# Keeping the split projection weights of a hybrid decoder block in DRAM between row blocks

## The chip, the core and the metric

The kernel runs on one core of a Trainium2 chip. A core has five engines that run their own instruction streams in order and meet at semaphores: PE (TensorE, matrix products), DVE (VectorE), ACT (ScalarE), POOL (GpSimd) and SP (SyncE), which here issues nearly all DMAs from one in-order queue. The metric is device time in microseconds (us) of a whole execution. The kernel before takes 1531.31 us, the median of three runs (1530.76, 1531.31 and 1535.02).

## The reference

One layer (DEPTH is 1) over 2048 rows of 1024 columns, in float32. What matters here is that all three mixers read one combined projection, with a weight matrix of 1024 rows and 4232 columns:

```
h = rms_norm(x, norm_g) * (1 + scale[:, None]) + shift[:, None]
proj = h @ w_in                       # 2048 x 1024 times 1024 x 4232
(ga_u, ga_v, ga_z, mb_q, mb_k, mb_v, mb_o, mb_z, mb_i, mb_f,
 sc_q, sc_k, sc_v, sc_z) = jnp.split(proj, offsets, axis=-1)
y_a = spatial_gating_branch(...) * silu(ga_z)      # gMLP, 4 groups of 64
h_b = mlstm_branch(...)                            # mLSTM, 4 heads of 96
y_c = stick_breaking_branch(...) * silu(sc_z)      # 6 heads of 64, strictly causal
y = jnp.concatenate([y_a, y_b, y_c], axis=-1) @ w_out
return x + gate[:, None] * y
```

The stick-breaking attention needs, for each query row, a running product over all earlier keys, so its work grows with the row's place in the sequence.

## The kernel before, in words

A row block is 5, 5 and 6 tiles of 128 rows (BLOCKS). For each block the normalised rows are turned once into hT, which holds a high part (float32 rounded to the PE's fp32r format) and a low part (what the rounding left). Then eleven groups of projection columns follow, of 384 columns each (392 for one): three for the attention (c_proj, p = 0 to 2), two for the mLSTM's q and k (bqk_proj), two for its gates (bg_proj), one each for its values (bv_proj) and the attention's gate (cz_proj), two for the gMLP (a_proj).

For every group of every block `weights` makes eight tiles "wr", one for 128 rows of w_in each, with a high and a low part. `load_w` fetches 256 rows into a staging tile "st" (two buffers). ACT copies each half into the high part (L180). Then DVE, for the even tile, or POOL, for the odd one, subtracts it from the staged values and so makes the low part (L181). A product of a tile of 128 rows is 8 steps of three matmuls (high by high, high by low, low by high), L285 to L287. The pool of "wr" tiles has 11 buffers: while one group is in use, three tiles of the next can be made ahead, and the tile of step k (from 3 on) has to wait until PE has done with step k - 3 of the group before, for the last row tile.

The attention of a pair of heads (`stick`) runs beside these groups: PE makes scores (L367, L368), ACT two sigmoids (L372, L373), DVE a running product (the scan, L380), DVE and POOL in turn a product (L384), PE turns it (L395), ACT and DVE split it (L397, L398), and PE multiplies by V (L410). The generators of `stick` are interleaved with those of the projections, and a scheduler puts the instructions of each engine into a fixed order by its own model of their times and by priorities; the weight work of later blocks has a high priority (HIGH is -4000). An engine runs its order without overtaking. K and V of the earlier blocks are kept in DRAM (k_d, v_d) and loaded again for each pair of heads.

The low-part line is the one whose engine alternates:

```
(nc.vector if a == 0 else nc.gpsimd).tensor_tensor(
    wt[:, 1, :W], st[:, a, :W], wt[:, 0, :W].bitcast(F32), ALU.subtract)
```

Of the kernel before, what the change touches and what calls it, by code (L numbers as in the profile page):

```python
# [8 lines left out]
F32 = mybir.dt.float32  # L9
F32R = mybir.dt.float32r  # L10
# [5 lines left out]
DRAM = bass.MemoryType.DRAM  # L16

P = 128
# [6 lines left out]
WMAX = 392  # L25
# [7 lines left out]
def hybrid_block_kernel(ctx: ExitStack, tc: tile.TileContext, x, c, norm_g, w_ada, b_ada, w_in,  # L33
# [8 lines left out]

# [1 line left out]
    qkT_d = dram.tile([768, SEQ], F32, name="qkT_d")  # L44
# [9 lines left out]

# [1 line left out]
    ident = const.tile([P, P], F32, name="ident")  # L56
# [35 lines left out]

# [1 line left out]
    rs = ExitStack()  # L94
# [50 lines left out]
    def mod_x(i, c0, c1, eng=None):  # L145
        """normalised and modulated, in place"""
        xc = x_cols(i, c0, c1)
        nc.vector.scalar_tensor_tensor(xc, xc, xtiles[i][1], hscale[:, c0:c1], ALU.mult, ALU.mult)
        (eng or nc.gpsimd).tensor_tensor(xc, xc, hshift[:, c0:c1], ALU.add)
# [10 lines left out]

    ntag = [0]

    def load_w(src, segs, kp):
# [8 lines left out]
    def weights(src, segs, kps=range(KT // 2), staged=None):  # L172
        """hi and lo parts of the given columns, one tile per 128 rows"""
        W = sum(w for _, w in segs)
        tiles = []
        for kp in kps:
            st = staged[kp] if staged else load_w(src, segs, kp)
            for a in range(2):
                wt = wr_p.tile([P, 2, WMAX], F32R, tag="wr", name=f"wr{ntag[0]}_{kp}_{a}")
                nc.scalar.copy(wt[:, 0, :W], st[:, a, :W])  # L180
                (nc.vector if a == 0 else nc.gpsimd).tensor_tensor(  # L181
                    wt[:, 1, :W], st[:, a, :W], wt[:, 0, :W].bitcast(F32), ALU.subtract)
                tiles.append(wt)
        ntag[0] += 1
        return tiles
# [4 lines left out]

# [1 line left out]
    ht_p = lw.enter_context(tc.tile_pool(name="ht", bufs=1))  # L192
# [51 lines left out]

# [1 line left out]
    NB0 = BLOCKS[0]  # L246
# [22 lines left out]
    def hT_half(i, j, hh):  # L269
        """half of the rows of tile j of hT, hi and lo parts"""  # L270
        cols = slice(j * P, (j + 1) * P)
        ks = slice(hh * 4, hh * 4 + 4)
        pt = (pat.tile([P, 4, P], F32, tag="at", name=f"pt{i}_{hh}") if i < BLOCKS[0] else
              pproj.tile([P, 512], F32, tag="proj", name=f"pt{i}_{hh}").rearrange("p (k t) -> p k t", k=4))
        for k in range(4):
            kk = hh * 4 + k
            nc.tensor.transpose(pt[:, k, :], x_cols(i, kk * P, (kk + 1) * P), ident)
        nc.scalar.copy(hT[:, 0, ks, cols], pt)
        nc.vector.tensor_tensor(hT[:, 1, ks, cols], pt, hT[:, 0, ks, cols].bitcast(F32), ALU.subtract)  # L279

    def proj_tc(ps, wt, j, W, ks=range(KT)):
        """psum[t, cols] of t tile j of the block"""
        cols = slice(j * P, (j + 1) * P)
        for k in ks:
            nc.tensor.matmul(ps, lhsT=hT[:, 0, k, cols], rhs=wt[k][:, 0, :W], start=k == 0, stop=False)  # L285
            nc.tensor.matmul(ps, lhsT=hT[:, 0, k, cols], rhs=wt[k][:, 1, :W], start=False, stop=False)  # L286
            nc.tensor.matmul(ps, lhsT=hT[:, 1, k, cols], rhs=wt[k][:, 0, :W], start=False, stop=k == KT - 1)  # L287
            yield 3 * W / 2.4

# [1 line left out]
    def c_proj(b, t0, nb, p):  # L291
# [148 lines left out]

# [1 line left out]
    def bqk_proj(t0, nb, half):  # L442
# [71 lines left out]

# [1 line left out]
    def a_proj(t0, nb, p):  # L516
# [37 lines left out]

# [1 line left out]
    def gating():  # L556
# [62 lines left out]

# [1 line left out]
    def bc4(ap, n):  # L621
# [31 lines left out]
    def first_chunk():  # L653
        """chunk 0 of the mLSTM ahead of the output phase: its gated output and the state after it"""
        big = [tmp.tile([P, D], F32, tag="xt", name=f"m0_{n}") for n in range(2)]
# [37 lines left out]

# [1 line left out]
    def gate_gemv():  # L695
# [137 lines left out]

# [1 line left out]
    rs.close()  # L835
# [46 lines left out]
    def mlstm(i):  # L882
        """numerator and denominator of chunk i, state after it"""
        qk2, vb = loaded[i][0:2]
        Cp = CT[0]
        wT = wk.tile([P, 4, P], F32, tag="wT", name=f"wT{i}")
        intra_weights(i, wT)
        pT = wk.tile([P, 4, P], F32, tag="pT", bufs=1, name=f"pT{i}")
        scores(psS.tile([P, 4, P], F32, tag="s", name=f"s{i}"), qk2, pT, wT)
        yield  # L890
        if i < NT - 1:
            kw = wk.tile([P, 4, 96], F32, tag="kw", bufs=1, name=f"kw{i}")
            weighted_k(i, psK.tile([P, 4, P], F32, tag="k", name=f"k{i}"), qk2, kw)
            yield
        ips = psI.tile([P, 4, P], F32, tag="i", name=f"i{i}")
        for h in range(4):
            nc.tensor.matmul(ips[:, h, 0:97], lhsT=qk2[:, h, :], rhs=Cp[:, h, :], start=True, stop=True)
        nd = wk.tile([P, 4, 97], F32, tag="nd", name=f"nd{i}")
        nc.vector.tensor_tensor(nd, ips[:, :, 0:97], bc4(ex[:, 0, 4 * i:4 * i + 4], 97), ALU.mult)
        yield  # L900
        nps = psN.tile([P, 4, P], F32, tag="n", name=f"n{i}")
        for h in range(4):
            nc.tensor.matmul(nps[:, h, 0:97], lhsT=pT[:, h, :], rhs=vb[:, h, :], start=True, stop=True)
        nc.vector.tensor_tensor(nd, nps[:, :, 0:97], nd, ALU.add)
        nds[i] = nd
        if i < NT - 1:
            yield
            cps = psK.tile([P, 4, P], F32, tag="k", name=f"c{i}")
            for h in range(4):
                nc.tensor.matmul(cps[0:96, h, 0:97], lhsT=kw[:, h, :], rhs=vb[:, h, :], start=True, stop=True)  # L910
            Cn = wk.tile([96, 4, 97], F32, tag="C", name=f"C{i}")
            nc.gpsimd.tensor_tensor(Cn, Cp, bc4(decay[0:96, 4 * i:4 * i + 4], 97), ALU.mult)
            nc.vector.tensor_tensor(Cn, cps[0:96, :, 0:97], Cn, ALU.add)
            CT[0] = Cn

    def mixed(i):
        """the gated outputs of the three mixers, [t, c]"""
        gt, y, xt = loaded[i][2:]
# [42 lines left out]
    def chunk_ahead(i):  # L961
        """chunk i from its scores to the turned outputs"""
        yield from mlstm(i)
        mixed(i)
        yield
        yield from turned(i)
# [66 lines left out]
```

## Time and profile before

| | |
|---|---|
| runs (us) | 1531.31 median, 1530.76 to 1535.02 |
| span of the profiled execution | 1527.0 us (the execution's own time is not given beside it; the runs are 3.8 to 8.0 us longer than this span) |
| busy: PE, DVE, POOL, ACT | 1413.2, 1123.3, 757.2, 749.6 us |
| granted clock of PE, mean | 0.978 |
| chain that ended last, by engine | PE 53%, DVE 25%, issue 7%, DMA 6%, POOL 5%, ACT 4% |
| DMA | 163.89 MB, 107 GB/s over the span |
| HBM read, written | 124.58 MB, 37.64 MB |

Busy is the union of an engine's instructions; matmuls overlap, so a busy PE is not a PE at its peak. After a start of about 62 us the projections of block 0 run to 354 us, those of block 1 to 718 us and those of block 2 to 1216 us; the attention of block 2 ends at 1264 us, and the output projection follows. The stretches 62 to 356, 356 to 720 and 720 to 1265 us stand for the three blocks. The weight tiles of block 1 are made from about 345 us on but for the first few, so the work on weights in blocks 1 and 2 is read from 345 to 1265 us.

### The profile page before, as it was taken

The numbers are of one execution on the slowest core, as the hardware profiler recorded it, in microseconds if no ns is written. First come the engines' busy times: TensorE is split into PE (matmuls) and PEld (weight loads), VectorE is DVE, ScalarE is ACT, GpSimd is POOL, SyncE is SP. The second block draws the span as 40 slices with busy tenths as digits, with TensorE's granted clock in tenths as the row PEclk, the third lists the DMA queues.
The fourth block names the chain that finished last, engine by engine and source line by source line (L and its number), as shares of the span: only waits on it lengthen the run. The fifth ranks groups of instructions, "written<-read, shape, count | busy, mean of one in ns | idle before, by whom it ended". The sixth has DMA issues, their size and how long they took to land.

```text
span 1527.0 us, 25375 instructions
## 1 busy us (share of the span) xinstructions
PE 1413.2 (93%) x8468; PEld 1307.1 (86%) x8468; DVE 1123.3 (74%) x1866; ACT 749.6 (49%) x1832; POOL 757.2 (50%) x1228
## 2 busy tenths in 40 slices
PE   5899999889889999988898899999998978999998
PEld 3789999889878999977898699989898956888887
DVE  6787555775997677699699986879968797544444
ACT  2365444454655455557366755656545565211210
POOL 4364544664445544666344554645535246534442
PEclk8899999999999999999999999999999999999999
DMA  9433423334435422523322124112230154546551
GB/s 325 130 92 100 121 80 87 95 109 122 133 93 140 136 69 74 141 53 111 103 63 74 41 63 124 46 48 76 78 89 18 62 189 120 196 128 190 149 158 67
DMA packets 170595, 163.89 MB, mean 107 GB/s; under 512 B 23610, under 2 KB 146904, under 8 KB 170464
## 3 DMA queue, kind: packets, MB, share of 16 engines
q1 hardware_dynamic: 170240, 162.24, 36.1%
q8 instruction: 67, 1.10, 0.3%
q14 instruction: 64, 0.52, 0.1%
q0 software_dynamic: 224, 0.02, 0.0%
HBM read 124.58 MB, written 37.64 MB: 106 GB/s over the span
## 4 chain that ended last, share of the span: by engine, by line
PE 53%; DVE 25%; issue 7%; DMA 6%; POOL 5%; ACT 4%; SPq 0%; DVEq 0%; POOLq 0%; ACTq 0%
DVE bb L380 9%; PE po L946 4%; PE po L948 4%; PE po L947 4%; PE av L410 3%; PE pc L287 3%; DMA st<-in_w_in_dram 3%; PE pc L285 3%; PE pc L286 3%; PE at L395 3%; DVE acc L467 2%; DVE aT L398 2%; PE pg L286 2%; DVE be L384 2%; PE pg L285 2%
## 5 line engine op out<-in xcount | busy, mean ns | idle before, releaser
L380 DVE TENSOR_TENSOR_SCAN bb<-bb,bb 128x513 f32<-128x513 f32 x144 | 198.9, 1382 | 18.4 <-ACT bb L372 18.0
L384 POOL TENSOR_TENSOR be<-be,bb 128x512 f32<-128x512 f32 (+3 forms) x120 | 135.3, 1127 | 125.2 <-DVE bb L380 65.5
L181 POOL TENSOR_TENSOR wr<-st,wr 128x384 fp32r<-128x384 f32 (+1 forms) x132 | 158.4, 1204 | 61.8 <-ACT wr L180 60.0
L180 ACT CAST wr<-st 128x384 fp32r<-128x384 f32 (+1 forms) x264 | 127.3, 522 | 113.0 <-DMA st<-in_w_in_dram 103.2
L410 PE MATMUL av<-aT,Vst 128*128 128x256 f32 x816 | 148.1, 298 | 30.4 <-DVE aT L398 20.8
L410 PEld LDWEIGHTS av<-aT,Vst 128*128 128x128 f32 x816 | 120.6, 192 | 47.5 <-DVE aT L398 30.5
L398 DVE TENSOR_TENSOR aT<-at,aT 128x512 fp32r<-128x512 f32 (+3 forms) x240 | 142.0, 596 | 24.0 <-ACT aT L397 23.6
L372 ACT ACTIVATE bb<-z 128x512 f32<-128x512 f32 (+3 forms) x240 | 131.1, 547 | 53.4 <-PE z L368 47.4
L397 ACT CAST aT<-at 128x512 fp32r<-128x512 f32 (+3 forms) x240 | 126.8, 529 | 51.7 <-PE at L395 50.4
L395 PE MATMUL at<-ident,be 128*128 128x128 f32 x816 | 133.3, 278 | 16.6 <-DVE Qst L340 7.3
L285 PE MATMUL pc<-wr,hT 128*128 128x384 f32 (+1 forms) x384 | 136.0, 356 | 7.2 <-DVE hT L279 6.2
L287 PE MATMUL pc<-wr,hT 128*128 128x384 f32 (+1 forms) x384 | 136.8, 356 | 2.6 <-DVE hT L279 2.6
L181 DVE TENSOR_TENSOR wr<-st,wr 128x384 fp32r<-128x384 f32 (+1 forms) x132 | 103.9, 787 | 47.8 <-ACT wr L180 47.5
L286 PE MATMUL pc<-wr,hT 128*128 128x384 f32 (+1 forms) x384 | 134.7, 351 | 0.0
L373 ACT ACTIVATE be<-z 128x512 f32<-128x512 f32 (+3 forms) x240 | 132.6, 552 | 0.0
L395 PEld LDWEIGHTS at<-ident,be 128*128 128x128 f32 x816 | 98.4, 142 | 28.2 <-DVE aT L398 11.1
L380 DVE TENSOR_TENSOR_SCAN bb<-bb 128x129 f32<-128x129 f32 (+3 forms) x96 | 95.7, 997 | 17.4 <-POOL bb L375 14.5
L946 PE MATMUL po<-wo,yT 128*128 128x512 f32 x256 | 104.8, 409 | 0.3 <-ACT yT L935 0.3
L947 PE MATMUL po<-wo,yT 128*128 128x512 f32 x256 | 102.3, 399 | 0.7 <-POOL wo L853 0.7
L948 PE MATMUL po<-wo,yT 128*128 128x512 f32 x256 | 101.4, 399 | 0.0
L371 POOL MEMSET bb<- 128x1 f32 x240 | 23.4, 98 | 150.6 <-DVE bb L380 98.8
L367 PE MATMUL z<-Kst,Qst 128*128 128x512 f32 (+3 forms) x240 | 93.7, 392 | 3.8 <-ACT be L373 3.7
(272 smaller groups left out, 4098.7 us busy)
## 6 DMA issues: line engine op xcount, KB each, us to landing
st<-in_w_in_dram SPq DMA_DIRECT2D x180, 128.0 KB, 2.4
st<-in_w_in_dram SPq DMA_DIRECT2D x48, 384.0 KB, 3.3
st<-in_w_in_dram SPq DMA_DIRECT2D x48, 192.0 KB, 2.6
wad<-in_w_ada_dram SPq DMA_DIRECT2D x8, 1024.0 KB, 7.3
xo<-in_x_dram SPq DMA_DIRECT2D x16, 512.0 KB, 3.6
out_dram<-o SPq DMA_DIRECT2D x31, 256.0 KB, 2.8
xt<-in_x_dram SPq DMA_DIRECT2D x15, 512.0 KB, 4.4
qk<-qkT_d SPq DMA_DIRECT2D x15, 384.0 KB, 7.5
```

Source lines behind the costliest of these rows:

```text
L181: (nc.vector if a == 0 else nc.gpsimd).tensor_tensor(wt[:, 1, :W], st[:, a, :W], wt[:, 0, :W].bitcast(F32), ALU.subtract)
L285: nc.tensor.matmul(ps, lhsT=hT[:, 0, k, cols], rhs=wt[k][:, 0, :W], start=k == 0, stop=False)
L286: nc.tensor.matmul(ps, lhsT=hT[:, 0, k, cols], rhs=wt[k][:, 1, :W], start=False, stop=False)
L287: nc.tensor.matmul(ps, lhsT=hT[:, 1, k, cols], rhs=wt[k][:, 0, :W], start=False, stop=k == KT - 1)
L380: nc.vector.tensor_tensor_scan(rev, rev, rev, carry.get((i, h), 1.0), ALU.mult, ALU.bypass)
L384: eng.tensor_tensor(be[:, :w], be[:, :w], bb[:, 1:w + 1], ALU.mult)
L395: nc.tensor.transpose(at[:, s, :], be[:, s * P:(s + 1) * P], ident)
L398: nc.vector.tensor_tensor(aT[:, :nb_, 1, :], at[:, :nb_, :], aT[:, :nb_, 0, :].bitcast(F32), ALU.subtract)
L410: nc.tensor.matmul(flat(av), lhsT=Vst[:, s0 + s, h, :], rhs=flat(aT[:, s]), start=(s0 + s == i), stop=(s0 + s == 0))
L946: nc.tensor.matmul(po, lhsT=yT[:, 0, k, :], rhs=wo[k][:, 0, cs], start=k == 0, stop=False)
L947: nc.tensor.matmul(po, lhsT=yT[:, 0, k, :], rhs=wo[k][:, 1, cs], start=False, stop=False)
L948: nc.tensor.matmul(po, lhsT=yT[:, 1, k, :], rhs=wo[k][:, 0, cs], start=False, stop=k == KT - 1)
```

## The change

In block 0 the tiles are made as before, and after each low part is made the whole tile (both parts) is also stored to a DRAM tensor of its own. `split` remembers these by the first column of the group and the tile's number. In blocks 1 and 2 a tile is not made again: a DMA loads both parts from DRAM straight into the "wr" tile. The staging load, the ACT copy and the subtraction are left out there. The number of "wr" buffers stays 11. Some comments are removed as well.

```
     ntag = [0]
+    split = {}
...
     def weights(src, segs, kps=range(KT // 2), staged=None):
         W = sum(w for _, w in segs)
         tiles = []
+        key = segs[0][0]
+        made = split.setdefault(key, {})
         for kp in kps:
+            if kp * 2 in made:
+                for k in (2 * kp, 2 * kp + 1):
+                    wt = wr_p.tile([P, 2, WMAX], F32R, tag="wr", name=f"wr{ntag[0]}_{k}")
+                    nc.sync.dma_start(wt[:, :, :W].bitcast(F32), made[k])
+                    tiles.append(wt)
+                continue
             st = staged[kp] if staged else load_w(src, segs, kp)
             for a in range(2):
                 wt = wr_p.tile([P, 2, WMAX], F32R, tag="wr", name=f"wr{ntag[0]}_{kp}_{a}")
                 nc.scalar.copy(wt[:, 0, :W], st[:, a, :W])
                 (nc.vector if a == 0 else nc.gpsimd).tensor_tensor(
                     wt[:, 1, :W], st[:, a, :W], wt[:, 0, :W].bitcast(F32), ALU.subtract)
+                made[2 * kp + a] = dram.tile([P, 2, W], F32, name=f"w_d{key}_{2 * kp + a}")
+                nc.sync.dma_start(made[2 * kp + a], wt[:, :, :W].bitcast(F32))
                 tiles.append(wt)
```

The scheduler orders all engines anew. The lines after the new ones move down by 11, so L167 is L168 in the changed kernel, L472 is L483, L501 is L512.

On SP in block 0, at the first group after the attention's (group number 2, bqk_proj; st2_3 is the load of its last 256 rows, wr2_1_1 its fourth tile). Before:

```order
L167 DMA st2_1_666<-in_w_in_dram 128x2x384
L167 DMA st2_2_674<-in_w_in_dram 128x2x384
L121 DMA xt5_3224<-in_x_dram 128x1024
L121 DMA xt6_3233<-in_x_dram 128x1024
L167 DMA st2_3_682<-in_w_in_dram 128x2x384
L167 DMA st3_0_1070<-in_w_in_dram 128x2x384
```

And now:

```order
L168 DMA st2_2_698<-in_w_in_dram 128x2x384
L355 DMA v_d0_71<-Vst_444 128x256 x2
L193 DMA w_d768_2_691<-wr2_1_0_688 256x1x384
L193 DMA w_d768_3_696<-wr2_1_1_693 256x1x384
L168 DMA st2_3_710<-in_w_in_dram 128x2x384
L354 DMA k_d0_68<-Kst_443 256x1x128
L355 DMA v_d0_71<-Vst_444 128x256
L193 DMA w_d768_4_703<-wr2_2_0_700 256x1x384
L193 DMA w_d768_5_708<-wr2_2_1_705 256x1x384
L354 DMA k_d0_68<-Kst_443 256x1x128
L168 DMA st3_0_1102<-in_w_in_dram 128x2x384
```

Two stores of whole tiles now stand ahead of each staging load.

On SP in block 1, between the first gate group (15) and the next (16, the attention's second pair of heads; gg is the gate product, stored by L501 or L512). Before:

```order
L501 DMA gate_d_62<-gg0_6_5582 128x192
L298 DMA Kst_427<-k_d1_69 128x2x512
L429 DMA y_d_63<-yc0_8_5574 128x128
L501 DMA gate_d_62<-gg0_7_5659 128x192
L167 DMA st16_3_5829<-in_w_in_dram 128x2x128 x3
L501 DMA gate_d_62<-gg0_8_5731 128x192
L167 DMA st17_0_6083<-in_w_in_dram 128x2x192 x2
```

And now:

```order
L512 DMA gate_d_62<-gg0_7_5755 128x192
L183 DMA wr16_3_5901<-w_d2824_3_1798 128x2x384
L512 DMA gate_d_62<-gg0_8_5827 128x192
L183 DMA wr16_4_5903<-w_d2824_4_1807 128x2x384
L183 DMA wr16_5_5905<-w_d2824_5_1812 128x2x384
L183 DMA wr16_6_5907<-w_d2824_6_1821 128x2x384
L183 DMA wr16_7_5909<-w_d2824_7_1826 128x2x384
L310 DMA Vst_444<-v_d1_72 128x256
L183 DMA wr17_0_6155<-w_d2112_0_2078 128x2x384
L183 DMA wr17_1_6157<-w_d2112_1_2083 128x2x384
L183 DMA wr17_2_6159<-w_d2112_2_2091 128x2x384
```

Where the staging load of the last quarter stood, the five loads of steps 3 to 7 stand now, with a gate store between the first and the second, and three loads for the group after behind them.

On ACT at the same place of block 1. Before:

```order
L496 ACTIVATE sgg0_6_5580<-pg0_6_5517 128x384
L180 CAST wr16_0_0_5803<-st16_0_5799 128x384
L180 CAST wr16_0_1_5806<-st16_0_5799 128x384
L372 ACTIVATE bb0_9_1_4_5635<-z0_9_1_4_5632 128x512
L180 CAST wr16_1_0_5813<-st16_1_5809 128x384
L414 COPY avs0_8_1_5525<-av0_8_1_5442 128x128
```

And now:

```order
L507 ACTIVATE sgg0_6_5676<-pg0_6_5613 128x384
L439 COPY yc0_8_5670<-py0_8_5667 128x128
L383 ACTIVATE bb0_9_1_4_5731<-z0_9_1_4_5728 128x512
L384 ACTIVATE be0_9_1_4_5732<-z0_9_1_4_5728 128x512
L408 CAST aT0_9_0_0_5709<-at0_9_0_0_5704 128x4x128
```

The weight copies are gone from among the sigmoids and the splits of the attention.

## Rows read from the trace of the kernel before

**Rows 1.** Busy time by stretch, the three blocks; columns as the head says.
```profile
core 0: us, PE busy (x) PEld busy (x) DVE busy (x) ACT busy (x) POOL busy (x), PEclk, DMA share, GB/s
62.00:356.00 294.00, 279.62 (x1716) 271.67 (x1715) 196.12 (x378) 148.52 (x407) 156.52 (x277) 0.98 0.35 96
356.00:720.00 364.00, 340.38 (x2106) 323.18 (x2104) 293.31 (x480) 202.75 (x511) 196.56 (x326) 0.99 0.38 107
720.00:1265.00 545.00, 505.01 (x3109) 472.56 (x3110) 452.41 (x710) 326.43 (x753) 252.75 (x453) 0.98 0.26 77
```

**Rows 2.** The chain that ended last, 345 to 1265 us, by line.
```profile
by line: DVE bb L380 12.8%; issue 7.9%; PE av L410 5.3%; PE at L395 4.2%; PE pc L285 3.9%; PE pc L287 3.8%; PE pc L286 3.8%; DVE aT L398 3.5%; DMA st<-in_w_in_dram 3.3%; DVE acc L467 3.3%; DVE be L384 3.2%; PE pg L286 2.2%; PE pg L285 2.2%;
```

**Rows 3.** The same chain, 62 to 345 us.
```profile
by line: DMA st<-in_w_in_dram 6.9%; issue 6.0%; DVE bb L380 5.7%; PE pg L286 5.0%; PE pg L287 5.0%; PE pg L285 4.9%; PE pc L287 4.1%; PE pc L286 3.9%; PE pc L285 3.8%; PE pb L453 3.1%; PE pb L454 2.8%; PE pb L455 2.8%; DVE wr L181 2.4%; PE 
```

**Rows 4.** Sum of five stretches: 400:475, 650:725, 775:900, 1050:1100, 1125:1175.
```profile
sum 375.00, PE 335.72 PEld 309.76 DVE 347.46 ACT 238.15 POOL 194.24; mean PE 67.14 PEld 61.95 DVE 69.49 ACT 47.63 POOL 38.85
```

**Rows 5.** The same five stretches, the wr tiles' work on DVE alone.
```profile
400.00:475.00 75.00, 5.26 (x8) 1.00 0.37 107
...
775.00:900.00 125.00, 6.75 (x9) 0.97 0.18 54
...
sum 375.00, DVE 24.21; mean DVE 4.84
```

**Rows 6.** Groups by line, 345 to 1265 us: count, busy us, mean ns, idle before.
```profile
L380 DVE TENSOR_TENSOR_SCAN bb<-bb,bb 128x513 f32<-128x513 f32 x138 | 191.2, 1386 | 16.1 <-ACT bb L372 15.7
...
L181 POOL TENSOR_TENSOR wr<-st,wr 128x384 fp32r<-128x384 f32 (+1 forms) x87 | 105.8, 1219 | 41.0 <-ACT wr L180 39.9
...
L180 ACT CAST wr<-st 128x384 fp32r<-128x384 f32 (+1 forms) x173 | 83.4, 525 | 66.7 <-DMA st<-in_w_in_dram 61.4 <-issue 3.2 <-PE z L368 1.2
...
L181 DVE TENSOR_TENSOR wr<-st,wr 128x384 fp32r<-128x384 f32 (+1 forms) x86 | 68.5, 796 | 24.7 <-ACT wr L180 24.6
```

**Rows 7.** Waits of ACT, 345 to 1265 us: total us, times, longest.
```profile
ACT wr L180 <- DMA st<-in_w_in_dram: 61.4, 39, 6.4
```

**Rows 8.** DMA issues, whole span: KB each, median us to landing.
```profile
st<-in_w_in_dram SPq DMA_DIRECT2D x180, 128.0 KB, 2.4
st<-in_w_in_dram SPq DMA_DIRECT2D x48, 384.0 KB, 3.3
...
v_d<-Vst SPq DMA_DIRECT2D x30, 128.0 KB, 1.7
...
gate_d<-sgz SPq DMA_DIRECT2D x16, 192.0 KB, 2.8
```

**Rows 9.** Timeline of PE, two steps of a projection with nothing between: start us, us.
```profile
344.63 0.34 PE L285 MATMUL pv<-wr,hT 128*128 128x384 f32 x1
344.81 0.34 PE L286 MATMUL pv<-wr,hT 128*128 128x384 f32 x1
344.99 0.34 PE L287 MATMUL pv<-wr,hT 128*128 128x384 f32 x1
345.16 0.34 PE L285 MATMUL pv<-wr,hT 128*128 128x384 f32 x1
345.34 0.33 PE L286 MATMUL pv<-wr,hT 128*128 128x384 f32 x1
345.51 0.34 PE L287 MATMUL pv<-wr,hT 128*128 128x384 f32 x1
```

**Rows 10.** Waits of the DMA queue, whole span: total us, times, longest.
```profile
SPq L472 <- DVE acc L470: 89.0, 27, 9.3
...
SPq L501 <- POOL gg L500: 28.7, 16, 5.3
```

**Rows 11.** One line's instructions, L181: duration ns min/median/max, first and last start.
```profile
L181 DVE TENSOR_TENSOR wr<-st,wr x132: 523/559/2755, 21.3 to 1176.1; 128x384 fp32r<-128x384 f32 x120, 128x392 fp32r<-128x392 f32 x12
```

**Rows 12.** The same of the scan, L380.
```profile
L380 DVE TENSOR_TENSOR_SCAN bb<-bb,bb x144: 1268/1278/3400, 114.7 to 1257.9; 128x513 f32<-128x513 f32 x144
```

More of the change, by code (lines that the diff above doesn't have):

```diff
@@ L161, in hybrid_block_kernel @@
     ntag = [0]
+    split = {}
     def load_w(src, segs, kp):
@@ L175, in weights @@
         tiles = []
+        key = segs[0][0]
+        made = split.setdefault(key, {})
         for kp in kps:
+            if kp * 2 in made:
+                for k in (2 * kp, 2 * kp + 1):
+                    wt = wr_p.tile([P, 2, WMAX], F32R, tag="wr", name=f"wr{ntag[0]}_{k}")
+                    nc.sync.dma_start(wt[:, :, :W].bitcast(F32), made[k])
+                    tiles.append(wt)
+                continue
             st = staged[kp] if staged else load_w(src, segs, kp)
@@ L182, in weights @@
                     wt[:, 1, :W], st[:, a, :W], wt[:, 0, :W].bitcast(F32), ALU.subtract)
+                made[2 * kp + a] = dram.tile([P, 2, W], F32, name=f"w_d{key}_{2 * kp + a}")
+                nc.sync.dma_start(made[2 * kp + a], wt[:, :, :W].bitcast(F32))
                 tiles.append(wt)
```

## The prediction

> **What bounds the kernel now.** I read the busy times by stretch first, then the chain that ended last, then the groups and waits that belong to the weight tiles. By stretch [rows 1] PE is busy 340 of 364 us in block 1 and 505 of 545 us in block 2, and DVE 293 (81%) and 452 us (83%). The reader is to see that PE comes first and DVE close behind, and that ACT and POOL have room. A matmul of 384 columns counts 0.34 us in that sum but the next one starts 0.175 us later [rows 9], so PE's busy time hides small holes, and the chain tells more: in blocks 1 and 2 its largest single line is DVE's scan with 12.8%, and a staging load of weights holds 3.3% [rows 2]. In block 0 that load is the largest of all, 6.9% [rows 3]. So three things count: DVE's time where DVE is full, the wait for a load, and whatever keeps PE's next weight tile away.
>
> **The change, part by part.**
>
> *Removed, in blocks 1 and 2:* 173 copies on ACT (83.4 us), 86 subtractions on DVE (68.5 us) and 87 on POOL (105.8 us) [rows 6]; the program has 176, 88 and 88, a few lie ahead of the stretch. ACT's and POOL's share lies beside other work, since both are near half busy; if that cover were not there the most that each could give is its own sum. DVE's share is worth something where DVE is the limit. I took the five stretches in which it is fullest, 375 us together: DVE is busy 347 us there, 93%, and PE 336 us, 90% [rows 4]. The subtractions in them are 24.2 us [rows 5]. PE is nearly as full, so I let two thirds come through: **16 us gained**. Bounds: 0 (PE takes over at once) and 68.5 us (every subtraction counts).
>
> *Removed with them, the wait for the staging load:* ACT stands still 61.4 us in 39 waits for it [rows 7], with the attention's sigmoids and splits queued behind. On the chain the load itself holds 3.3% of 920 us, **30 us** [rows 2]. What is late next is the load that takes its place.
>
> *Added, in blocks 1 and 2:* 176 loads of 384 KB instead of half as many bytes, straight into the weight tiles. Tiles 0 to 2 of a group have free buffers and come early. Tiles 3 to 7 wait for PE to leave steps 0 to 4 of the group before, and PE needs each of them ten steps later: 10 x 3 x 0.175 = 5.3 us if only projections stand between [rows 9]. One load of 384 KB lands after 3.3 us, one of 128 KB after 2.4 [rows 8], so 256 KB more cost 0.9 us and a load behind another costs 1.35 us. Buffers come free every 0.53 us, the fifth 2.1 us after the first; it lands at about 3.3 + 4 x 1.35 = 8.7 us and is wanted at 2.1 + 5.3 = 7.4. A bare transition would thus stall PE 1.3 us. Few are bare: a group holds 5 x 8 x 3 x 0.175 = 21 us of projections in block 1 and 25 in block 2, but takes 364/11 = 33 and 545/11 = 50 us [rows 1], so the 5.3 us stretch to 8 and 11 us. What remains is SP, whose queue doesn't overtake: in the new order a gate store stands between the loads of tiles 3 and 4, in other groups the store of a convolved tile. Such stores hold SP 28.7/16 = 1.8 us and 89.0/27 = 3.3 us a time [rows 10]; behind them wait the loads, and PE for those. The cost of a transition is bounded by 0 and 3.3 us; I take 0.8, the part of 1.8 that the room of about 1 us doesn't cover. For 22 groups that is **18 us lost**, so the two waits together gain 30 - 18 = 12 us. Bounds for the pair: 30 gained, 73 - 30 = 43 lost.
>
> *Added in block 0:* 88 stores of 384 KB. The trace has no such store. A store of 128 KB from the same memory lands after 1.7 us and one of 192 KB after 2.8, near the loads of that size [rows 8], so I give it a load's 1.35 us in the queue. Two stand ahead of each staging load now. Three of a group's four loads are fetched long ahead; the last one is gated and becomes 2.7 us later, which for ten groups is at most 27 us. The load is on the chain there already, 6.9% of 283 us, 20 us [rows 3], which speaks for a real cost. But the block's DMA share is only 0.35, and DVE and ACT are at 67% and 51% [rows 1], so the split behind it can catch up. I take a good third: **10 us lost**; bounds 0 and 27. The stores hold weight buffers a little longer, which costs nothing as PE uses those for far longer than a store takes.
>
> *A page weighed against a row.* DVE's subtraction has a median of 559 ns but a longest of 2755 [rows 11], and the scan 1278 against 3400 [rows 12]: something holds both up at times. The Trainium skill, SBUF — State Buffer, section "Who interferes with whom", says that a DVE instruction with two SBUF inputs contends with a GpSimd one that reads SBUF, and that the second waits for the first. The long tails agree with it, though the rows don't name the other side. By that rule POOL's subtractions also lengthen DVE work that stays.
>
> *Sum.* -16 - 12 + 10 = -18 us. The profiled span is 1527.0 us; the runs lie 4 us above it at the median, and what surrounds the span isn't touched. So 1527.0 - 18 = 1509 in the span and **1513 us** as a run.
>
> **The rivals.**
>
> *More comes free (1485 us).* The loads come early enough and POOL's subtractions were slowing DVE. The mean of a full scan is 1386 ns against a median of 1278 [rows 6, 12]: 138 x 0.108 = 15 us. POOL's weight work is 105.8 of some 450 us that POOL is busy there [rows 1, 6], about a quarter, so 4 us are its own by share; all 24.2 us of DVE come through; the 30 us of load wait go, less 4 of stalls; block 0 pays 8. That is -4 - 24 - 26 + 8 = -46, so 1485 us. For it: DVE's 93% [rows 4]. Against it: PE is as good as full in the same stretches.
>
> *PE waits for the new loads (about 1565 us).* SP reaches each gated load late, behind a store whose data DVE or POOL finishes late. At 3.3 us for each of 22 transitions 73 us are lost; with the rest as forecast, 73 - 30 - 16 + 10 = +37, 1568 us. It decides from (30 + 16 - 10)/22 = 1.6 us a transition on. For it: 1.8 us is what a gate store holds SP already. Against it: in these blocks PE has other work for half of the time.
>
> *Block 0 takes it back (1530 us).* The full 27 us there, the rest as forecast: -16 - 12 + 27 = -1. For it: the load leads the chain of that block [rows 3]. Against it: only one load in four is gated.
>
> That the tiles are not reused at all can be left out: the order shows the loads in place of copies and subtractions.
>
> **How the numbers follow.** A run tells 0.3% from no change, 4.6 us here. The forecast, taken as 1495 to 1526 us, gets 0.50; more comes free 0.18; PE waits 0.18; block 0 takes it back 0.14, of which about 0.09 falls within 4.6 us and 0.05 above. Faster by over 0.3% is 0.50 + 0.18 = 0.68, less 0.02 for the forecast's upper edge, 0.66; within 0.3% 0.09 + 0.02 = 0.11; slower 0.18 + 0.05 = 0.23. The range that leaves two in ten out goes from 1483 (just past the gain rival) to 1545 us (a mean stall of 2.3 us a transition, between the point where the slower rival decides and its bound).
>
> **What would show it right or wrong.** Right: ACT's and POOL's busy time falls by about 83 and 106 us, DVE's by 70 to 90; the staging load leaves the chain between 345 and 1265 us; PE's waits for a weight load sum to 10 to 25 us over some 22 groups; block 0 ends some 10 us later and blocks 1 and 2 together are some 28 us shorter. Wrong: PE's waits for those loads sum to over 40 us, with SP held by gate or convolution stores just before; or block 0 grows by over 20 us with ACT's wait for the staging load in it; or DVE falls as said and blocks 1 and 2 don't get shorter, so that DVE was not what they waited for.

## The result and the profile after

The changed kernel takes **1479.86 us**, the median of 4 runs (1477.62 to 1482.68), against 1533.16 us (1530.76 to 1535.09, 4 runs) for the kernel before on the same chip: ratio 0.9658, 95% interval [0.9637, 0.9679], 3.4% faster. The forecast was 1513 us with a range from 1483, so the direction was right and the gain nearly three times too small. The profiled execution took 1480.27 us with a span of 1478.5 us, 48.5 us shorter than the span before. Below, a ratio r of an experiment is turned into microseconds over the changed kernel as (r - 0.9658) x 1532.

The page of the changed kernel: busy time, share of the span and instructions of each engine; then the chain that ended last, by engine; then three groups of DMA issues (KB each, median us to landing).

```profile
PE 1400.6 (95%) x8468; PEld 1302.7 (88%) x8468; DVE 1025.1 (69%) x1778; ACT 678.1 (46%) x1656; POOL 647.3 (44%) x1140
...
PE 68%; DVE 16%; DMA 5%; issue 4%; POOL 3%; ACT 3%; SPq 1%; DVEq 0%; POOLq 0%; ACTq 0%
...
wr<-w_d SPq DMA_DIRECT2D x160, 384.0 KB, 5.6
w_d<-wr SPq DMA_DIRECT2D x80, 384.0 KB, 3.5
...
st<-in_w_in_dram SPq DMA_DIRECT2D x60, 128.0 KB, 3.7
```

PE held 53% of the chain before and holds 68% now, DVE 16% instead of 25%. ACT's busy time fell by 71.5 us, POOL's by 109.9, DVE's by 98.2 (forecast 83, 106 and 70 to 90). The new loads land after 5.6 us, not the 3.3 us that staging loads of that size took before [rows 8], and the staging load of 128 KB after 3.7 us instead of 2.4.

Busy time in the three blocks, cut where the attention of each ends now (columns as in [rows 1]):

```profile
62.00:352.00 290.00, 276.55 (x1695) 267.50 (x1693) 191.55 (x374) 145.86 (x403) 155.60 (x274) 0.98 0.66 214
352.00:694.00 342.00, 335.92 (x2110) 323.15 (x2110) 245.54 (x434) 167.28 (x422) 139.21 (x281) 1.00 0.49 162
694.00:1217.00 523.00, 497.88 (x3117) 469.64 (x3116) 412.39 (x669) 293.56 (x671) 204.21 (x414) 0.99 0.34 112
```

Against [rows 1] the blocks are 4, 22 and 22 us shorter. PE's idle time fell from 24 to 6 us in block 1 and from 40 to 25 us in block 2. Block 0, with its 88 stores, has a DMA share of 0.66 instead of 0.35 and is not longer.

The chain in blocks 1 and 2 (345 to 1217 us) by line, to hold against [rows 2]:

```profile
by line: DVE bb L391 9.0%; PE av L421 6.9%; PE at L406 6.1%; PE pc L296 5.3%; PE pc L298 5.2%; PE pc L297 5.1%; issue 4.0%; PE pg L298 3.2%; PE pg L297 3.2%; PE pg L296 3.2%; PE z L378 2.8%; PE z L379 2.8%; DVE aT L409 2.5%; DVE be L395 2.4
```

The staging load is gone from it, the scan fell from 12.8% to 9.0% and "issue" from 7.9% to 4.0%; PE's lines took their place. The largest wait of ACT there is now for PE, and PE hardly waits for the new loads (total us, times, longest us; PEld is PE's weight load):

```profile
ACT aT L408 <- PE at L406: 62.8, 92, 2.8
```

```profile
PE pb L464 <- DMA wr<-w_d: 0.6, 2, 0.3
...
PEld pb L464 <- DMA wr<-w_d: 1.9, 4, 0.6
PEld pc L296 <- DMA wr<-w_d: 0.3, 1, 0.3
```

The PE row lies at the same moments as the PEld rows, so PE's queue stands for 2.2 us in all over 22 groups, where the forecast had 18. In the kernel before, PE stood for weight tiles too, for the copy or the subtraction: 7.8 us in five such rows (345 to 1265 us; the longest three):

```profile
PEld pv L286 <- DVE wr L181: 2.7, 1, 2.7
PEld pg L286 <- DVE wr L181: 2.0, 1, 2.0
PEld pb L455 <- DVE wr L181: 1.4, 2, 1.3
```

SP still stands for the convolved tiles and the gate products before it can store them, and longer a time than in [rows 10] (3.8 and 2.1 us instead of 3.3 and 1.8; whole span):

```profile
SPq L483 <- DVE acc L481: 102.5, 27, 11.1
...
SPq L512 <- POOL gg L511: 25.3, 12, 3.8
```

### The profile page after: what moved, and what is told of

It is laid out like the page before. It is cut to its first block, busy times and chain, and to the rows that moved or that the text cites. A ratio compares the mean times of both kernels' runs of the same rounds, so it can differ in the third digit from the quotient of the medians.

```text
span 1478.5 us, 24942 instructions
## 1 busy us (share of the span) xinstructions
PE 1400.6 (95%) x8468; PEld 1302.7 (88%) x8468; DVE 1025.1 (69%) x1778; ACT 678.1 (46%) x1656; POOL 647.3 (44%) x1140
## 4 chain that ended last, share of the span: by engine, by line
PE 68%; DVE 16%; DMA 5%; issue 4%; POOL 3%; ACT 3%; SPq 1%; DVEq 0%; POOLq 0%; ACTq 0%
DVE bb L391 6%; PE av L421 5%; PE pc L296 4%; PE pc L298 4%; PE at L406 4%; PE pc L297 4%; PE po L957 4%; PE po L959 3%; PE po L958 3%; PE pg L298 3%; PE pg L297 3%; PE pg L296 3%; PE pb L465 2%; PE pb L464 2%; PE z L378 2%
## 5 line engine op out<-in xcount | busy, mean ns | idle before, releaser
L391 DVE TENSOR_TENSOR_SCAN bb<-bb,bb 128x513 f32<-128x513 f32 x144 | 194.1, 1348 | 24.9 <-ACT bb L383 23.8
L409 DVE TENSOR_TENSOR aT<-at,aT 128x512 fp32r<-128x512 f32 (+3 forms) x240 | 142.7, 597 | 31.5 <-ACT aT L408 30.5
L391 DVE TENSOR_TENSOR_SCAN bb<-bb 128x129 f32<-128x129 f32 (+3 forms) x96 | 86.9, 905 | 23.5 <-POOL bb L386 16.3
L466 PE MATMUL pb<-hT,wr 128*128 128x320 f32 (+1 forms) x288 | 91.9, 324 | 2.4 <-DVE wr L190 2.4
L464 PE MATMUL pb<-hT,wr 128*128 128x320 f32 (+1 forms) x288 | 93.1, 324 | 0.6 <-DMA wr<-w_d 0.6
L465 PE MATMUL pb<-hT,wr 128*128 128x320 f32 (+1 forms) x288 | 92.2, 322 | 0.0
```

The costliest lines, as they stand in the source:

```text
L391: nc.vector.tensor_tensor_scan(rev, rev, rev, carry.get((i, h), 1.0), ALU.mult, ALU.bypass)
L409: nc.vector.tensor_tensor(aT[:, :nb_, 1, :], at[:, :nb_, :], aT[:, :nb_, 0, :].bitcast(F32), ALU.subtract)
```

## The experiments

Three accounts of the gain stood against each other. First, that it comes from the queues of ACT, DVE and POOL: each runs in order, and work on weights that waits there for a load or for another engine holds up the masks, scans, products and splits of the attention behind it. Second, that it comes from PE getting its weight tiles sooner. Third, that it comes from DVE's time alone, as the forecast's term of 16 us had it. The edits are shown against the changed kernel.

**The stores alone.** Block 0 as changed, later blocks as before.

```diff
-            if kp * 2 in made:
+            if False:
...
+                if 2 * kp + a not in made:
```

> Block 0 stores its 88 tiles as in the changed kernel, but blocks 1 and 2 fetch, copy and subtract as before: the stores alone. The forecast had them cost 10 us (bounds 0 and 27): 1543 us, with block 0's last projection about 10 us later than 354 us. The rival after seeing the changed kernel (its block 0 ends at 350 us): the stores are hidden, 1533 us within 5 and block 0 no later than 356 us.

1533.11 us, ratio 1.0009 [0.9993, 1.0024] over 10 runs. Block 0 ends no later (62 to 354 us here, 62 to 356 before) at the DMA share of the changed kernel:

```profile
62.00:354.00 292.00, 276.05 (x1697) 266.12 (x1696) 193.45 (x376) 148.40 (x408) 160.36 (x278) 0.99 0.66 209
```

The 88 stores cost 4 us at the upper end of the interval and 1 at its middle, so the 10 us of the forecast are not there.

**Half of the tile from DRAM.** In one kernel only the low part is stored and loaded (staging load and ACT copy stay, no subtraction); in another only the high part (no ACT copy, subtractions stay).

```diff
+                if k in made:
+                    nc.sync.dma_start(wt[:, 1, :W].bitcast(F32), made[k])
+                else:
...
```

> Blocks 1 and 2 keep the staging load and ACT's copy of the high part; only the low part is loaded from DRAM (192 KB a tile, stored in block 0), so the 88 subtractions on DVE and 88 on POOL go and nothing else. Theory A, the subtractions' time on DVE and POOL is what came free: most of the 53 us, 1485 to 1500 us. Theory B, it was ACT's wait for the staging load with the attention queued behind: little, 1520 to 1530 us, since that wait is still there.

1513.89 us, 0.9897 [0.9876, 0.9919]: 16 of the 53 us, between what the two theories had. ACT still stands 66.1 us for the staging load:

```profile
ACT wr L184 <- DMA st<-in_w_in_dram: 66.1, 34, 5.3
```

```diff
+                if k in made:
+                    nc.sync.dma_start(wt[:, 0, :W].bitcast(F32), made[k])
+                else:
...
```

> The other half: blocks 1 and 2 load the high part from DRAM (192 KB a tile), keep the staging load, and DVE and POOL still subtract; ACT's 176 copies go, and with them ACT's wait for the staging load. Theory A (the subtractions count): 1522 to 1533 us. Theory B (ACT's wait counts): 1490 to 1505 us. If both count by halves, 1505 to 1520 us here and in the run with the low part alone.

1564.63 us, 1.022 [1.0196, 1.0245]: 33 us slower than the kernel before, which no expectation held. DVE and POOL now wait for two loads each, 105 us of the two engines together (waits of POOL, then of DVE, 345 to 1265 us):

```profile
POOL wr L190 <- DMA wr<-w_d: 45.0, 28, 3.4
...
POOL wr L190 <- DMA st<-in_w_in_dram: 10.3, 11, 2.6
```

```profile
DVE wr L190 <- DMA st<-in_w_in_dram: 29.1, 23, 3.3
...
DVE wr L190 <- DMA wr<-w_d: 20.8, 12, 4.7
```

PE's own waits for weight tiles stay below 5 us. This kernel has less work on ACT than the one before and is slower, so here what DVE and POOL wait for at the head of their queues counts for more than the work taken from ACT.

**One engine's subtractions put back.** The changed kernel, with subtractions on the loaded tiles whose result nobody reads: 88 on DVE, 88 on POOL, or 176 copies on ACT.

```diff
+                    if k % 2 == 0:
+                        junk = stg_p.tile([P, 2, WMAX], F32, tag="st", name=f"jk{ntag[0]}_{k}")
+                        nc.vector.tensor_tensor(junk[:, 0, :W], wt[:, 0, :W].bitcast(F32), wt[:, 1, :W].bitcast(F32), ALU.subtract)
```

> The changed kernel with 88 subtractions of 128x384 put back on DVE in blocks 1 and 2 (of the loaded tile's two parts, into a staging tile that nothing reads). Theory A, DVE's time counts in full where DVE is near 93% busy: 24 us or more come back, 1500 to 1515 us. Theory B, DVE has room once ACT doesn't wait: at most 8 us, 1480 to 1488 us.

DVE: 1504.95 us, 0.9839 [0.9805, 0.9873], 28 us over the changed kernel, as theory A had it.

> The changed kernel with 88 subtractions of 128x384 put back on POOL in blocks 1 and 2 (of the loaded tile's two parts, into a staging tile that nothing reads). If POOL's reads hold up DVE's instructions with two inputs in SBUF and the attention's products on POOL wait behind it: 1490 to 1505 us. If POOL has room, as its 44% busy says: 1480 to 1486 us.

POOL (the same with `k % 2` and `nc.gpsimd`): 1517.16 us, 0.9896 [0.9866, 0.9925], 36 us, more than either expectation, on an engine that is busy 44% of the time in the changed kernel.

> The changed kernel with 176 copies of 128x384 put back on ACT in blocks 1 and 2 (from the loaded tiles into staging tiles that nothing reads). The bare wait on ACT (88 tiny copies) cost 12 us; the low part alone loaded, with ACT's copies and staging loads kept, left 34 us of the gain away. If ACT's own work counts as DVE's and POOL's does: 1500 to 1515 us. If only its wait counts: 1488 to 1496 us.

ACT (`nc.scalar.copy(junk[:, 0, :W], wt[:, 0, :W].bitcast(F32))` for every tile): 1493.47 us, 0.9748 [0.9722, 0.9774], 14 us for 89.8 us of copies, as expected if only the wait counts. In the kernel with the low part alone, ACT's staging loads and copies, kept, left 37 us of the gain away: what one engine's queue costs seems to depend on the others.

**One engine's wait alone.** The same places, but each instruction touches 8 columns of the loaded tile.

```diff
+    tiny = const.tile([P, 8], F32, name="tiny")
...
+                    if k % 2 == 0:
+                        nc.vector.tensor_tensor(tiny, wt[:, 0, 0:8].bitcast(F32), wt[:, 1, 0:8].bitcast(F32), ALU.subtract)
```

> The other half of the same: 88 subtractions of 128x8 on DVE that read the loaded tiles, so that DVE waits for every second load as before but does hardly any work. Theory W: 1480 to 1487 us. Theory Q: 1495 to 1505 us.

DVE: 1496.85 us, 0.9765 [0.9741, 0.979], 16 us, as theory Q had it.

> The changed kernel with 88 subtractions of 128x8 on POOL that read the loaded tiles: POOL waits for every second load in its queue and does hardly any work. The full subtractions on POOL cost 35 us, with 67 us of waiting for loads. If it is POOL standing before a load, with the attention's masks and products behind it: 1500 to 1515 us. If it is the 1.15 us of each subtraction: 1480 to 1492 us.

POOL: 1492.87 us, 0.9756 [0.9727, 0.9785], 15 us, between the two ranges.

> The changed kernel with 88 copies of 128x8 on ACT that read the loaded tiles: ACT waits for every second load, with the attention's sigmoids and splits behind it, as it waited for the staging loads before, and does hardly any work. If that wait was worth the 30 us that the load had on the chain: 1500 to 1510 us. If ACT's order has room for it: 1480 to 1487 us.

ACT (a copy of 8 columns for every second tile): 1492.43 us, 0.975 [0.9725, 0.9775], 14 us, again between the two. The groups in the three kernels, 345 to 1265 us (busy us, mean ns, idle before):

```profile
L186 DVE TENSOR_TENSOR tiny<-wr 128x8 f32<-128x8 f32 x86 | 24.1, 280 | 58.6 <-DMA wr<-w_d 58.4
```

```profile
L186 POOL TENSOR_TENSOR tiny<-wr 128x8 f32<-128x8 f32 x87 | 25.4, 292 | 100.5 <-DMA wr<-w_d 93.2 <-PE at L409 4.9 <-DVE bb L394 1.8
```

```profile
L186 ACT COPY tiny<-wr 128x8 f32<-128x8 f32 x86 | 17.4, 203 | 94.9 <-DMA wr<-w_d 94.6
```

Some 17 to 25 us of work cost 14 to 16 us, because each engine idles 58 to 95 us at the head of its queue. For ACT the full copies cost no more than the wait. For DVE the work adds some 12 us, for POOL some 21.

**The control.** 88 memsets of 8 columns on POOL, which wait for nothing.

```diff
+                    if k % 2 == 0:
+                        nc.gpsimd.memset(tiny, 0.0)
```

> A control: the changed kernel with 88 memsets of 128x8 on POOL in blocks 1 and 2 that wait for nothing, so that the scheduler orders the program anew and hardly any work is added (88 x 0.1 us). If a new order by itself moves the time: anything between 1470 and 1500 us. If the costs seen so far are those of the work and the waits: 1476 to 1484 us.

1483.17 us, 0.9679 [0.966, 0.9698]: 3 us. It is a weaker control than it was meant to be, because the scheduler put all 88 at the start, ahead of block 0:

```profile
L186 POOL MEMSET tiny<- x88: 94/104/109, 7.4 to 36.0; 128x8 f32 x88
```

From 345 us on, 99% of DVE's instructions stand in the order that they have in the changed kernel (by the timelines, the added memsets and subtractions left out), so the control doesn't show what a new order costs by itself, and no run does. The other kernels speak against it as the cause: DVE's bare wait keeps 97% of the order and costs 16 us, ACT's copies keep 78% and cost 14.

**DVE's work without a wait.** 88 subtractions of resident tiles.

```diff
...
+                        nc.vector.tensor_tensor(junk[:, 0, :W], hscale[:, :W], hshift[:, :W], ALU.subtract)
```

> The changed kernel with 88 subtractions of 128x384 on DVE in blocks 1 and 2 that read two resident tiles, so that DVE does the work but waits for no load (the result goes to a staging tile that nothing reads). The run with the subtractions of loaded tiles took 1505 us, 25 more than the changed kernel, with 50 us of DVE waiting for loads. Theory W, it is DVE's time: 1495 to 1505 us here. Theory Q, it is DVE standing in its queue before a load: 1480 to 1488 us here.

1515.11 us, 0.9887 [0.9871, 0.9903], 35 us, above both theories. It doesn't answer its question cleanly: with nothing to wait for, the scheduler put all of them between 318 and 507 us (first view: one line's instructions; second: stretches, columns as in [rows 1]).

```profile
L186 DVE TENSOR_TENSOR jk<-hscale,hshift x88: 521/549/1483, 318.0 to 507.2; 128x384 f32<-128x384 f32 x80, 128x392 f32<-128x392 f32 x8
```

```profile
400.00:450.00 50.00, 42.52 (x260) 37.94 (x259) 49.11 (x88) 26.16 (x63) 21.53 (x39) 0.93 0.35 112
450.00:500.00 50.00, 38.41 (x228) 35.46 (x229) 47.92 (x92) 18.51 (x44) 14.73 (x26) 0.93 0.35 114
```

DVE is full there and PE falls to 81 of 100 us: of some 88 x 0.55 = 48 us of work added to a full DVE, 35 us come through.

**POOL's time without its reads.** After the 8-column wait, a memset of the whole staging tile, so POOL is busy as long as in the kernel with the subtractions, but reads nothing large.

```diff
+                        nc.gpsimd.tensor_tensor(tiny, wt[:, 0, 0:8].bitcast(F32), wt[:, 1, 0:8].bitcast(F32), ALU.subtract)
...
+                        nc.gpsimd.tensor_scalar(junk[:, 0, 0:8], tiny, 1.0, None, ALU.mult)
+                        nc.gpsimd.memset(junk, 0.0)
```

> The changed kernel with POOL busy for about the time of a subtraction after every second load, but without reading SBUF in that time: a tiny subtraction and a tiny copy that wait for the load, then a memset of 128x784. The full subtraction on POOL cost 37 us, the bare wait 13. Theory port (a POOL instruction that reads SBUF holds up DVE's instructions with two SBUF inputs): little more than the bare wait, 1490 to 1498 us. Theory queue (the attention's masks and products wait behind it on POOL): 1508 to 1520 us.

1506.73 us, 0.9825 [0.9795, 0.9855], 26 us: between the bare wait (15) and the subtractions (36), and between the two theories, nearer to the queue. The page's first line of three kernels, POOL with subtractions, POOL with memsets, POOL with the wait alone:

```profile
PE 1417.3 (94%) x8468; PEld 1310.3 (87%) x8468; DVE 1046.1 (69%) x1778; ACT 675.6 (45%) x1656; POOL 759.0 (50%) x1228
```

```profile
PE 1410.4 (94%) x8468; PEld 1303.8 (87%) x8468; DVE 1028.0 (68%) x1778; ACT 678.2 (45%) x1656; POOL 767.6 (51%) x1404
```

```profile
PE 1407.6 (94%) x8468; PEld 1306.4 (88%) x8468; DVE 1023.8 (69%) x1778; ACT 676.5 (45%) x1656; POOL 665.6 (45%) x1228
```

DVE runs the same 1778 instructions in each and in the changed kernel (1025.1 us). With POOL's subtractions beside them they take 21 us longer, with even more POOL time in memsets only 3. What POOL's queue does to DVE is seen in the scan's wait for POOL's mask, 345 to 1265 us, in the changed kernel, with the wait alone, with the memsets and with the subtractions:

```profile
DVE bb L391 <- POOL bb L386: 10.9, 19, 1.9
```

```profile
DVE bb L394 <- POOL bb L389: 18.2, 22, 2.9
```

```profile
DVE bb L397 <- POOL bb L392: 31.9, 27, 4.0
```

```profile
DVE bb L394 <- POOL bb L389: 24.3, 20, 3.2
```

A mask is a 0.3 us instruction, but it stands behind whatever POOL has before it.

**Everything put back.** Loads and stores as changed, PE free of the three engines, and 176 copies on ACT, 88 subtractions on DVE and 88 on POOL on the loaded tiles, each subtraction behind its copy as in the kernel before, results unread.

```diff
...
+                    nc.scalar.copy(junk[:, a, :W], wt[:, 1, :W].bitcast(F32))
+                    (nc.vector if a == 0 else nc.gpsimd).tensor_tensor(
+                        junk[:, a, :W], wt[:, 0, :W].bitcast(F32), junk[:, a, :W], ALU.subtract)
```

> The changed kernel with all three kinds of work put back in blocks 1 and 2, on the loaded tiles and into a staging tile that nothing reads: 176 copies on ACT, 88 subtractions on DVE and 88 on POOL, each subtraction behind its copy. Only the way of the products is new: PE waits for the load and not for a subtraction. One kind alone cost 25 us (DVE) and 35 us (POOL). Theory S, the engines' queues are all of the gain and share it: 1525 to 1540 us. Theory P, PE no longer waiting for the subtractions is a good part: 1505 to 1520 us. If the parts added up: over 1560 us.

1535.84 us, 1.002 [1.0008, 1.0032], 55 us: the whole gain is gone, as theory S had it. The waits are those of the kernel before (ACT 61.4 for the load, POOL 39.9 and DVE 24.6 for ACT [rows 6, 7]), somewhat longer; waits of ACT, POOL and DVE, 345 to 1265 us:

```profile
ACT jk L186 <- DMA wr<-w_d: 71.8, 70, 4.5
```

```profile
POOL jk L187 <- ACT jk L186: 52.8, 34, 4.1
```

```profile
DVE jk L187 <- ACT jk L186: 25.8, 22, 5.2
```

PE does not wait for this work at all. So the first account holds. The second falls: PE gains by sooner tiles at most the 7.8 us that it stood for them before, and here that is nil or paid back by the longer waits. The third falls too, as POOL's work alone costs more than DVE's. PE's clock is not the cause either: granted in the mean 0.978 to 0.983 of its full level in these runs, 0.973 to 0.978 in the runs of the kernel before beside them, which take the same time. Alone, the three engines cost 28 + 36 + 14 = 78 us, together 55: an engine that is late hides that another is.

**Room for the loads.** Eight weight buffers instead of eleven, so that no tile of a group can be loaded ahead.

```diff
-    wr_p = lw.enter_context(tc.tile_pool(name="wr", bufs=11))
+    wr_p = lw.enter_context(tc.tile_pool(name="wr", bufs=8))
```

> The changed kernel with 8 buffers for the weight tiles in place of 11: no tile of the next group can come early, and each has eight steps, 8 x 0.53 = 4.2 us of bare projections, between its buffer coming free and its use, in place of ten; a load lands after 5.6 us in the median. If the room of ten steps and three early tiles is what hides the loads: PE's waits for them show, 1.5 to 3 us in each of 22 transitions, 1510 to 1545 us. If the attention between the steps hides them anyway: 1480 to 1490 us.

1489.65 us, 0.9727 [0.9707, 0.9748], 11 us, in the range for waits that the attention hides. PE's queue now stands 12.5 us for the new loads (five rows of PEld; the three rows of PE, 6.5 us, lie at the same moments; the longest three):

```profile
PE pc L296 <- DMA wr<-w_d: 3.3, 5, 1.5
```

```profile
PEld pc L296 <- DMA wr<-w_d: 5.4, 6, 1.8
PEld pb L464 <- DMA wr<-w_d: 4.8, 7, 1.9
```

That is 0.6 us for each of 22 groups, not far from the 0.8 that the forecast had charged with eleven buffers.

**Two attempts at a faster version.** In block 2 the tile of step 3 goes into the staging buffers, which stand empty there; and blocks of 4, 6 and 6 tiles.

```diff
+                    if k == 3 and ntag[0] >= 23:
+                        wt = stg_p.tile([P, 2, WMAX], F32R, tag="st", name=f"ws{ntag[0]}_{k}")
```

> A version meant to be faster: in block 2 the staging buffers, which nothing uses there any more, take each group's tile of step 3, so that seven tiles a group share the 11 buffers and four or five come early. If the loads' waits on the chain (about 8 us in block 2) are worth something: 1472 to 1478 us. If they are hidden anyway: 1478 to 1484 us.

1478.49 us, 0.9648 [0.9631, 0.9666]: the same as the changed kernel within the intervals. Earlier loads gain nothing where PE doesn't wait for them.

```diff
-BLOCKS = [5, 5, 6]
+BLOCKS = [4, 6, 6]
```

> A version meant to be faster: row blocks of 4, 6 and 6 tiles in place of 5, 5 and 6. Only block 0 still splits weights, and with fewer row tiles it has less of the attention's work beside it; blocks 1 and 2 use each load for six tiles. If the split in block 0 hinders the attention: 1465 to 1478 us. If block 0 gets too short to cover the split (11 groups of 24 x 0.175 x 4 = 17 us each): 1485 to 1510 us.

1502.36 us, 0.9806 [0.9778, 0.9834], 23 us slower than the changed kernel. No version tried beats it by more than the intervals.

## Why the prediction was wrong

The direction was right, and the time came from where the forecast looked, blocks 1 and 2; the size was wrong. By the spans the forecast was -18 us and the result -48.5, a miss of 30.5.

- **"18 us lost", the new loads' stalls.** This step failed: 2.2 us of waits. What failed is the 0.8 us a transition for the gate stores ahead of the loads in SP's queue: I set their 1.8 us a time against the shortest room alone. SP stands 2.1 us a time for them now and the loads land after 5.6 us, yet PE hardly waits, so the room is larger than what I left of it; how large wasn't measured. With eight buffers a price of that size is there (0.6 us), with eleven it isn't.
- **"10 us lost", block 0's stores.** This step failed: 1.0009 with the stores alone, and block 0 is 4 us shorter. The staging load did become later (3.7 us instead of 2.4) and still holds 4.8% of the chain there, less than the 6.9% before. A wait on the chain is no proof that lengthening it by 1 us a time is paid in full. These two losses are most of the 30.5 us, 16 from the loads and 10 from the stores; why block 0 shrank by 4 us on top is open.
- **"16 us gained" (DVE) and the 30 us of staging wait.** Their sum of 46 is not far from the 55 us that putting all of it back costs, but that is in part luck, as the split is not what the runs show. DVE's subtractions put back alone cost 28 us, of which 16 come with the bare wait at their head, which had no term; their work adds some 12. ACT's wait, 30 us on the chain, is worth 14 put back alone.
- **"ACT's and POOL's share lies beside other work".** For ACT's work this held: 89.8 us of copies cost no more than their wait. This step failed for POOL: its subtractions stood at nothing in the sum, and put back they cost 36 us at 44% busy. The bare wait is 15 of them; time in the queue, with memsets, brings 26; the subtractions 36. The last 10 go with the 18 us by which DVE's same 1778 instructions lengthen from memsets to subtractions.
- **The page weighed.** The Trainium skill, SBUF — State Buffer, section "Who interferes with whom", sets a GpSimd instruction that only writes SBUF apart from one that reads it, and gives only the latter a conflict with a two-input DVE instruction. The runs agree: 1028.0 us of DVE beside memsets, 1046.1 beside subtractions. So does the timeline of the kernel before, 345 to 1265 us, among the instructions that it shows singly: 71 full scans with no POOL instruction beside them but memsets took 1.29 us at most, the 64 with one beside them 1.51 in the mean and up to 3.40, the tail of [rows 12]. DVE's subtractions took 0.93 us in the mean beside one of POOL's (46) and 0.56 at most with no reading POOL instruction beside them (10). `aT<-at,aT`, which has one input in PSUM (where PE puts its results) and not in SBUF (the core's working memory), took 0.68 either way. In the forecast I told the rule and gave it no term in the sum. DVE's busy time fell by 98 us, of which its subtractions are some 71 (132 of them, 103.9 us, before; 44, 33.0 us, now); the rest is other instructions that got shorter, the scans among them (246 in all, 296.0 and 283.2 us by their groups), which fits.
- **The rivals.** "More comes free" (1485 us, given 0.18) is nearly what happened, in part by luck: it has DVE in full, few stalls and POOL's drag on DVE, but it lacks POOL's own queue and still pays 8 us for the stores. "PE waits for the new loads" and "block 0 takes it back" fell with the two losses.

Left open: in the POOL kernels the granted clock is 0.975 with subtractions and 0.981 with memsets, so part of the 10 us between them may be PE's clock and not DVE's lengthening; but the one run with subtractions at 0.987 took 1510.1 us, more than any run with memsets (at most 1508.7, at 0.980). What a new order of the instructions costs by itself wasn't measured either. What DVE's work costs spread out and without a wait wasn't measured, as the scheduler bunched it. The put-back work waits for loads that land later than the staging loads did, so 28, 36 and 14 are each engine's price in the changed kernel, not exactly what it cost before.

## What to carry to other kernels

The busy share of an engine off the critical path doesn't price work put into its queue: in a loop that hops between engines (mask, scan, product, split), price queued work by the wait at its head and by what stands behind it, here 14 to 16 us for 88 nearly empty instructions that wait. Put work back unread, one engine at a time and then all together; the sum of the singles (78 us) against the whole (55 us) tells how far they hide each other. Don't charge a transfer twice: once its room covers its landing it costs nothing more, and heavier traffic alone cost nothing measurable here, up to a DMA share of 0.66 in block 0. Look also at where a control's instructions come to stand before trusting it.

## What the runs showed of the hardware

- The new loads of 384 KB, up to eight in a row in SP's queue, land after 5.6 us at the median (all 176: 3.3 to 8.8), where the staging loads of that size took 3.3 before, and the stores of the same size after 3.5; a staging load of 128 KB among these stores took 3.7 us instead of 2.4.
- The same 1778 DVE instructions took 1025.1 us in all, 1046.1 beside 88 POOL subtractions of two SBUF inputs, and 1028.0 beside memsets that kept POOL busy longer. In the kernel before, a full scan, which has two SBUF inputs, took 1.29 us at most with no reading POOL instruction beside it and 1.51 in the mean with one; a DVE subtraction with one input in PSUM took 0.68 us in either case.
